# A two-layer decoder trunk on one core: VectorE in program order, weight units split two ahead, and the first four projection tiles summed slice by slice of x

## The chip, the core and the metric

The kernel runs on one core of a Trainium2 chip. The metric is device time in microseconds (us): the median of the runs of one program. One more execution is profiled, and its trace is what the rows below come from.

## The reference, cut to what matters

The input x is 256 tokens of 2048 values; all data are fp32. Two layers follow one another, and a last RMSNorm closes the program:

```python
for l in range(2):
    h = rmsnorm(x, mix_norm_g[l])
    pa, pb, pc, pd = split(h @ w_in[l])            # one projection, four groups of columns
    ya = gated_mlp(pa)                             # layer norm over v, causal 128x128 mixing
    yb = rwkv7(pb)                                 # p += (previous token - p) * mu, then the delta rule
    yc = block_attention(pc)                       # rotary q and k, softmax
    yd = gated_linear_attention(pd)
    x = x + concat(ya, yb, yc, yd) @ w_out[l]
    u = causal_conv3(rmsnorm(x, ffn_norm_g[l]) @ w_up[l])
    gate, up = split(u)
    x = x + (silu(gate) * up) @ w_down[l]          # inner width 5632
return rmsnorm(x, final_norm_g)
```

## The kernel before, in words

**Weights.** All weights come as one stream `ws` of 776 units; a unit is 128 x 1024 fp32 (512 KB) and holds 8 blocks of 128 x 128. SP issues the loads into 4 buffers `raw`. Each unit is split in two halves: ScalarE casts a half to H (fp32r, L182), VectorE subtracts, L = raw - H (L183); H and L have 7 buffers each. TensorE makes three products for each block, H with the high part of the activation, H with its low part, L with the high part (L219 to L221; wide forms L206 to L209 and L240 to L242). `proj` sums 16 blocks, that is two units, to one tile of 128 x 256 in PSUM.

**Order.** Only TensorE's order is the written one. The other engines' instructions are placed by a scheduler; the splits carry a priority of 3000, so they go in front of whatever else is ready on ScalarE and VectorE. Each call of `unit()` (L173) splits the unit and calls `pump()` (L150), which runs one step of each live generator: the mixers' work (`b_pre`, `b_grams`, `b_vt`, `solve`, `d_scores`, `c_rope`, `c_score`, `a_mix`) is written as generators, and TensorE gets a step's matmuls between two units.

**Start.** x is loaded in four pieces of 4 slices (a slice is 128 features of all 256 tokens), the first piece in two halves with the halves of unit 0 between; then come units 1 to 5 and a table `cst`. `x_ready` (L248) turns a slice into its high part on ScalarE (L255) and its low part on VectorE (L90, the helper `stt`). `x_square` (L258) sums the squares for the norm on ScalarE and VectorE, some odd slices on GpSimd; `rms_gen` (L286) sums them over features on TensorE (L293), takes the power on GpSimd (L298) and spreads the row scale to `rb` (L304, L306). Four projection tiles follow one another, each summed over all 16 slices, units 0 to 7.

**Group B of the projection.** `shift` (L348) is one token's mixing with the one before: VectorE multiplies by `rb` (L351), ScalarE scales (L352), VectorE adds the shifted part (L90). The first tiles go to `act12`, `pm13`, k and r, then v. `b_pre` (L375) prepares decay and gates, `b_grams` (L480) makes the norms: a reduction (L505), a transfer to DRAM (`tN`, L508) and back (L511) issued by GpSimd, and then 15 pairs of a product (L518) and a sum (L520), growing from 1 to 225 elements. `solve` (L567) inverts by squaring: matmul (L576), product (L591), add (L595).

**Feed-forward.** For each of 44 inner tiles a round makes two wide projections, `conv` on each (VectorE L1070, ScalarE L1072, two L90 on VectorE), Silu, a product (L1101), and the split of the result (L1103, L1104).

Of the kernel before, what the change touches and what calls it, by code (L numbers as in the profile page):

```python
# [10 lines left out]
F32 = mybir.dt.float32  # L11
# [41 lines left out]
def trunk_kernel(ctx: ExitStack, tc: tile.TileContext, x, ws, ph, pf, pm, pa, pb, cs, out, depth=DEPTH):  # L53
    nc = tc.nc
# [70 lines left out]
    for n in range(2, 4):  # L125
        raws[n] = load_raw(n)
    for n in range(4, 6):
        raws[n] = load_raw(n)
# [42 lines left out]
    ust = {"u": 0, "ev": None, "blk": 8, "H": None, "L": None}  # L171

    def unit():  # L173
        u = ust["u"]
        raw = raws.pop(u) if u in raws else load_raw(u)
        H, L = [], []
        for n in range(2):
# [7 lines left out]
            L.append(l)  # L185
        ust["u"] = u + 1
        ust["blk"] = 0
        ust["H"], ust["L"] = H, L
        pump()
        return H, L  # L190

    def block():
# [3 lines left out]
        ust["blk"] = b + 1  # L196
        w = slice((b % 4) * 128, (b % 4 + 1) * 128)
# [60 lines left out]
    def x_square(k, pool=False, final=False):  # L258
# [61 lines left out]
    with tc.high_priority(offset=3000):  # L320
        for k in range(16):
            x_ready(k, phs[0], PF_MIXG)
    with tc.high_priority(offset=2962):
        for k in range(16):
            x_square(k, True)

    for layer in range(depth):
# [958 lines left out]
```

## Time and profile before

| | us |
|---|---|
| median of 3 runs | 2379.26 |
| lowest and highest | 2378.59, 2380.8 |
| profiled execution | 2378.92 |
| its span in the trace | 2377.2 |
| TensorE busy | 2354.7 (99%) |
| VectorE busy | 1765.9 (74%) |
| ScalarE busy | 1349.5 (57%) |
| GpSimd busy | 99.4 (4%) |

The span runs from the first to the last instruction; 1.72 us of the execution lie around it. A busy share is an average over stages, and matmul ends are modelled. The times at which TensorE starts its instructions, and the waits that the trace puts down to a releaser, say where it loses time.

### The profile page before, as it was taken

Reading aid. Unit: us, or ns where it says so; the run is one execution under the profiler, and the core shown is the slowest. Engines: PE = TensorE matmul, PEld = TensorE weight load, DVE = VectorE, ACT = ScalarE, POOL = GpSimd, SP = SyncE. Lnnn points to the kernel's source line nnn. Section 1 sums busy time; section 2 is a strip of 40 time slices with the busy share of each in tenths; the row PEclk is TensorE's granted clock in tenths of the full one; section 3 lists DMA queues with packets and bytes.
Section 4 is the critical chain, followed back from the end, with each engine's and each line's share of the span. In section 5 each row is a group of like instructions: output and inputs, shape, how many; then the busy total and the mean of one; then the engine's idle time right before and its main releaser. Section 6 shows DMA issues by size and latency. Waiting matters only on the chain.

```text
span 2377.2 us, 39934 instructions
## 1 busy us (share of the span) xinstructions
PE 2354.7 (99%) x14764; PEld 2058.6 (87%) x14764; DVE 1765.9 (74%) x3471; ACT 1349.5 (57%) x2605; POOL 99.4 (4%) x134
## 2 busy tenths in 40 slices
PE   8999999999999999999999999999999999999998
PEld 8987888988888888888899788889888888888887
DVE  7886677787875588787668867777888756788764
ACT  6654456566654466665565444556666545666654
POOL 3110100000000000000011011000000000000000
PEclk9999999999999999999999999999999999999999
DMA  7553455555555555555655434455555555555553
GB/s 242 172 180 105 140 180 186 187 186 186 186 186 191 191 186 186 187 186 199 208 176 185 152 107 166 171 186 187 186 186 186 186 188 187 190 188 187 185 180 132
DMA packets 117859, 426.81 MB, mean 180 GB/s; under 512 B 13376, under 2 KB 13520, under 8 KB 117536
## 3 DMA queue, kind: packets, MB, share of 16 engines
q1 hardware_dynamic: 114144, 412.38, 50.0%
q0 software_dynamic: 3520, 11.89, 1.8%
q8 instruction: 115, 1.88, 0.3%
q14 instruction: 80, 0.66, 0.1%
HBM read 419.50 MB, written 4.72 MB: 178 GB/s over the span
## 4 chain that ended last, share of the span: by engine, by line
PE 98%; DVE 1%; DMA 0%; ACT 0%; issue 0%; POOL 0%; SPq 0%; POOLq 0%; ACTq 0%; DVEq 0%
PE mm L207 47%; PE mm L206 23%; PE mm L240 4%; PE mm L242 4%; PE mm L241 4%; PE mm L219 3%; PE mm L221 3%; PE mm L220 3%; PE mm L209 1%; PE mx L642 1%; PE mx L576 1%; PE mx L541 1%; DMA ab<-in_x_dram 0%; PE mx L923 0%; PE mx L832 0%; PE mx L952 0%
## 5 line engine op out<-in xcount | busy, mean ns | idle before, releaser
L182 ACT CAST H<-raw 128x512 fp32r<-128x512 f32 x1552 | 959.0, 620 | 916.0 <-PE mm L207 654.0
L183 DVE TENSOR_TENSOR L<-raw,H 128x512 fp32r<-128x512 f32 x1552 | 1074.9, 694 | 521.5 <-ACT H L182 503.5
L207 PE MATMUL mm<-xa,H 128*128 128x512 f32 x3008 | 1050.0, 397 | 0.0
L206 PE MATMUL mm<-xa,L 128*128 128x256 f32 x2820 | 792.9, 281 | 0.0
L207 PEld LDWEIGHTS mm<-xa,H 128*128 128x128 f32 x3008 | 553.1, 188 | 120.6
L207 PE MATMUL mm<-s,H 128*128 128x512 f32 x1560 | 544.1, 395 | 0.1
L206 PEld LDWEIGHTS mm<-xa,L 128*128 128x128 f32 x2820 | 531.6, 188 | 8.8
L206 PE MATMUL mm<-s,L 128*128 128x256 f32 x1470 | 413.1, 281 | 0.0
L207 PEld LDWEIGHTS mm<-s,H 128*128 128x128 f32 x1560 | 286.9, 188 | 60.8 <-DVE s L1104 1.0
L206 PEld LDWEIGHTS mm<-s,L 128*128 128x128 f32 x1470 | 277.4, 189 | 4.1
L90 DVE SCALAR_TENSOR_TENSOR w1k<-w1k,pft,w1k 128x255 f32<-128x255 f32 x352 | 169.1, 480 | 13.4
L240 PE MATMUL mm<-H,xa 128*128 128x512 f32 x384 | 159.4, 415 | 0.0
L219 PE MATMUL mm<-xa,H 128*128 128x256 f32 x512 | 150.0, 293 | 7.2 <-ACT H L182 6.3
L242 PE MATMUL mm<-L,xa 128*128 128x512 f32 x384 | 152.4, 397 | 0.0
L241 PE MATMUL mm<-H,xa 128*128 128x512 f32 x384 | 152.1, 396 | 0.0
L221 PE MATMUL mm<-xa,L 128*128 128x256 f32 x512 | 146.2, 286 | 1.2 <-DVE L L183 1.2
L220 PE MATMUL mm<-xa,H 128*128 128x256 f32 x512 | 146.5, 286 | 0.3 <-DVE xa L90 0.3
L219 PEld LDWEIGHTS mm<-xa,H 128*128 128x128 f32 x512 | 98.7, 193 | 8.0 <-ACT H L182 6.3
L1072 ACT ACTIVATE w1k<-w1k,pft 128x256 f32<-128x256 f32 x176 | 104.8, 595 | 0.1
L221 PEld LDWEIGHTS mm<-xa,L 128*128 128x128 f32 x512 | 98.6, 192 | 1.8 <-DVE L L183 1.8
L220 PEld LDWEIGHTS mm<-xa,H 128*128 128x128 f32 x512 | 98.6, 192 | 1.3 <-DVE xa L90 1.0
L240 PEld LDWEIGHTS mm<-H,xa 128*128 128x128 f32 x384 | 72.5, 189 | 20.8 <-issue 3.6
(298 smaller groups left out, 2165.5 us busy)
## 6 DMA issues: line engine op xcount, KB each, us to landing
raw<-in_ws_dram SPq DMA_DIRECT2D x775, 512.0 KB, 3.3
s<-in_pb_dram POOLq DMA_DIRECT2D x10, 256.0 KB, 5.3
ab<-in_x_dram POOLq DMA_DIRECT2D x4, 512.0 KB, 6.0
xscr<-ab POOLq DMA_DIRECT2D x4, 512.0 KB, 5.0
ab<-xscr POOLq DMA_DIRECT2D x4, 512.0 KB, 5.9
ab<-in_x_dram SPq DMA_DIRECT2D x3, 512.0 KB, 8.4
out_dram<-s SPq DMA_DIRECT2D x3, 512.0 KB, 4.5
cst<-in_cs_dram SPq DMA_DIRECT2D x1, 1040.5 KB, 7.2
```

Of the source, the lines that this page charges most:

```text
L90: return V.scalar_tensor_tensor(out=o, in0=a, scalar=s, in1=b, op0=op0, op1=op1)
L182: S.copy(h, src)
L183: V.tensor_sub(l, src, h.bitcast(F32))
L206: T.matmul(ps[:, :256], L, a[:, 0, :], start=False, stop=False)
L207: T.matmul(ps, H, a.rearrange("p s n -> p (s n)"), start=(k == 0), stop=(k == n - 1))
L219: T.matmul(o, H, a[:, 0, :], start=(k == 0), stop=False)
L220: T.matmul(o, H, a[:, 1, :], start=False, stop=False)
L221: T.matmul(o, L, a[:, 0, :], start=False, stop=(k == n - 1))
L240: T.matmul(ps[t], ah[:, ts], H[k % 2], start=(k == 0), stop=False)
L241: T.matmul(ps[t], al[:, ts], H[k % 2], start=False, stop=False)
L242: T.matmul(ps[t], ah[:, ts], L[k % 2], start=False, stop=(k == n - 1))
L1072: S.activation(acc, hr, AF.Identity, scale=cw(2), bias=cw(3))
```

## The change

1. VectorE joins TensorE in the written order: what stands in the program first runs first, and a priority no longer moves anything on it.
2. The split is a function of its own, `split(u)`; `unit()` takes a split that is made already, pumps the mixers, and then splits ahead up to two units (`look`, 2 after the first four tiles, 0 before).
3. x comes in pieces of 1, 1, 2, 2, 2, 4 and 4 slices between the units. `first_tiles()` sums four tiles slice by slice, in two banks of PSUM; the program that prepares the weights reorders the first units so that each holds the blocks of two slices for four tiles. Squares are taken two slices at a time on ScalarE and added on VectorE; the squares on GpSimd go. Ten fp32 matmuls on a zeroed tile stand ahead of everything on TensorE.
4. In layer 0 `rms_gen` starts one step earlier in units of half the length (`fine`), the tables `hb` and `selrk` are made behind it, and the tiles of `act12`, `pm13`, k0 and k1 are the first four, k2 the fifth.
5. Steps of mixers move: `b_pre`'s scans wait for k3; the exponentials of `b_grams`' input are fetched one ahead; `b_vt` has a wait more; `d_scores`' preparation has two parts; the softmax's scaling comes a step later (`c_scale`); `a_mix` has one yield between its power and its use of it; in the feed-forward the product and the split of round j come inside round j+1 (`gate2`, `gate3`), and both convolutions stand behind the second projection.

```diff
-    load_x(1, x, nc.sync)
-    raws[1] = load_raw(1)
-    for n in range(2, 4):
-        load_x(n, x, nc.sync)
...
+    for n in range(1, 4):
+        first_x(2 * n, 2)
         raws[n] = load_raw(n)
+    for c in range(2, 4):
+        first_x(4 * c, 4)
...
+    busy = slot("s13", [256])
+    V.memset(busy, 0.0)
...
-    ctx.enter_context(tc.manual_schedule(engines={mybir.EngineType.PE}))
+    ctx.enter_context(tc.manual_schedule(engines={mybir.EngineType.PE, mybir.EngineType.DVE}))
+    wps = mx()
+    for n in range(10):
+        T.matmul(wps[:, :128], busy[:, :128], busy[:, 128:256], start=True, stop=True)
...
+    def unit():
+        u = ust["u"]
+        if u not in splits:
+            split(u)
         ust["u"] = u + 1
         ust["blk"] = 0
-        ust["H"], ust["L"] = H, L
+        H, L = ust["H"], ust["L"] = splits.pop(u)
         pump()
+        for v in range(u + 1, min(u + 1 + ust["look"], 2 * depth * NW)):
+            if v not in splits:
+                split(v)
         return H, L
...
+        for k in range(16):
+            if k % 2 == 0:
+                ready(k + 2)
+                split(k // 2 + 1)
+                ready(k + 3)
+                with tc.high_priority(offset=2962):
+                    x_square2(k, acc)
+            hls = [block() for n in range(4)]
+            if k < 14:
+                for n in range(4):
+                    step(n, k, hls[n])
+            else:
+                late.append(hls)
+        for n in range(4):
+            for d in range(2):
+                step(n, 14 + d, late[d][n])
+        ust["look"] = 2
...
-        o = proj(xacts())
-        o13 = proj(xacts())
-        ok0 = proj(xacts()) if layer == 0 else None
+        early = list(outs0) if layer == 0 else []
...
+        early += [proj(xacts()) for _ in range(1 if layer == 0 else 2)]
+        ust["fine"] = False
         drain(gR)
+        o, o13 = next_b(), next_b()
...
-                ga = conv(pg, 2 * j)
-                ua = conv(pu, 2 * j + 1)
+                cg, cu = conv(pg, 2 * j), conv(pu, 2 * j + 1)
+                ga, ua = conv2(*cg), conv2(*cu)
                 S.activation(ga, ga, AF.Silu)
-                V.tensor_mul(ga, ga, ua)
                 gt[j] = gcur[:, jj]
-                S.copy(gt[j][:, 0, :], ga)
-                V.tensor_sub(gt[j][:, 1, :], ga, gt[j][:, 0, :].bitcast(F32))
+                pend = (j, ga, ua)
```

**VectorE at the start.** Before, a row is L90 for a slice's low part, L183 for a weight half and L274 for a sum of squares:

```order
L90 SCALAR_TENSOR_TENSOR xa_111<-ab_1_79,pht_76,xa_111 128x256 x2
L183 TENSOR_TENSOR L_224<-raw_80,H_223 128x512
L90 SCALAR_TENSOR_TENSOR xa_116<-ab_1_79,pht_76,xa_116 128x256 x2
L183 TENSOR_TENSOR L_228<-raw_80,H_227 128x512
L274 TENSOR_TENSOR acc_19_151<-acc_19_151,w1k_155 128x256
L90 SCALAR_TENSOR_TENSOR xa_121<-ab_3_85,pht_76,xa_121 128x256 x2
L90 SCALAR_TENSOR_TENSOR xa_126<-ab_3_85,pht_76,xa_126 128x256 x2
L183 TENSOR_TENSOR L_256<-raw_87,H_255 128x512
```

After, L194 is the weight half and L287 the sum of squares of two slices:

```order
L90 SCALAR_TENSOR_TENSOR xa_129<-ab_1_79,pht_76,xa_129 128x256
L194 TENSOR_TENSOR L_133<-raw_83,H_132 128x512
L194 TENSOR_TENSOR L_137<-raw_83,H_136 128x512
L90 SCALAR_TENSOR_TENSOR xa_129<-ab_1_79,pht_76,xa_129 128x256
L90 SCALAR_TENSOR_TENSOR xa_142<-ab_1_79,pht_76,xa_142 128x256
L194 TENSOR_TENSOR L_146<-raw_89,H_145 128x512
L194 TENSOR_TENSOR L_150<-raw_89,H_149 128x512
L90 SCALAR_TENSOR_TENSOR xa_142<-ab_1_79,pht_76,xa_142 128x256
```

Weight halves and slices alternate from the first slice on, two halves for two slices, where slices 4 to 15 stood before the second and third unit's halves.

**VectorE behind the first tiles.** Before, L351 and L90 are a shift's two steps, L749 to L759 copies and fills for the gates, and L183 stands between them:

```order
L351 TENSOR_TENSOR w1k_438<-mm_222,rb_429 128x256
L183 TENSOR_TENSOR L_586<-raw_583,H_585 128x512
L183 TENSOR_TENSOR L_590<-raw_583,H_589 128x512
L90 SCALAR_TENSOR_TENSOR s_44_213<-w1k_438,pft_197,s_44_213 128x256
L351 TENSOR_TENSOR w1k_448<-mm_287,rb_429 128x256
L183 TENSOR_TENSOR L_636<-raw_633,H_635 128x512
L749 COPY s_44_213<-s_44_213 32x256
L96 TENSOR_SCALAR sg_215<-s_44_213 96x256
L90 SCALAR_TENSOR_TENSOR s_44_213<-w1k_448,pft_197,s_44_213 128x256
L183 TENSOR_TENSOR L_640<-raw_633,H_639 128x512
```

After, the shift's steps are L409 and L90, its first column's fill L408:

```order
L408 MEMSET w1k_607 128x1
L409 TENSOR_TENSOR w1k_607<-mm_128,rb_539 128x256
L90 SCALAR_TENSOR_TENSOR s_75_470<-w1k_607,pft_463,s_75_470 128x256
L408 MEMSET w1k_613 128x1
L409 TENSOR_TENSOR w1k_613<-mm_128,rb_539 128x256
L90 SCALAR_TENSOR_TENSOR s_75_470<-w1k_613,pft_463,s_75_470 128x256
L408 MEMSET w1k_619 128x1
L409 TENSOR_TENSOR w1k_619<-mm_482,rb_539 128x256
L90 SCALAR_TENSOR_TENSOR s_75_470<-w1k_619,pft_463,s_75_470 128x256
L194 TENSOR_TENSOR L_629<-raw_626,H_628 128x512
```

Five shifts, from the one of `act12` (eleven rows further up) to the one of k2 (`w1k_619`), stand in one row ahead of the halves of unit 12 (`L_629` and the next).

**VectorE around unit 46 of layer 0.** Before, L884 to L890 are the rotary step of one input (two tokens' halves), and the norms' pairs L518 and L520 are long done:

```order
L884 TENSOR_TENSOR w2k_2027<-mm_1749,rope_433 128x512
L885 TENSOR_TENSOR w2k_2028<-mm_1749,rope_433 128x512
L183 TENSOR_TENSOR L_2137<-raw_2134,H_2136 128x512
L889 TENSOR_TENSOR s_402_2026<-w2k_2027,w2k_2028 128x8x32
L890 TENSOR_TENSOR s_402_2026<-w2k_2028,w2k_2027 128x8x32
L884 TENSOR_TENSOR w2k_2033<-mm_1750,rope_433 128x512
L183 TENSOR_TENSOR L_2141<-raw_2134,H_2140 128x512
L885 TENSOR_TENSOR w2k_2034<-mm_1750,rope_433 128x512
L183 TENSOR_TENSOR L_2177<-raw_2174,H_2176 128x512
L889 TENSOR_TENSOR s_402_2026<-w2k_2033,w2k_2034 128x8x32
```

After, L976 to L982 are the rotary step, L584 and L586 the norms' pairs:

```order
L194 TENSOR_TENSOR L_1993<-raw_1990,H_1992 128x512
L194 TENSOR_TENSOR L_1997<-raw_1990,H_1996 128x512
L976 TENSOR_TENSOR w2k_2013<-mm_1748,rope_583 128x512
L977 TENSOR_TENSOR w2k_2014<-mm_1748,rope_583 128x512
L981 TENSOR_TENSOR s_397_2012<-w2k_2013,w2k_2014 128x8x32
L982 TENSOR_TENSOR s_397_2012<-w2k_2014,w2k_2013 128x8x32
L976 TENSOR_TENSOR w2k_2019<-mm_1749,rope_583 128x512
L977 TENSOR_TENSOR w2k_2020<-mm_1749,rope_583 128x512
L981 TENSOR_TENSOR s_397_2012<-w2k_2019,w2k_2020 128x8x32
L982 TENSOR_TENSOR s_397_2012<-w2k_2020,w2k_2019 128x8x32
L584 TENSOR_TENSOR w1k_2028<-s_322_1710 128x81
L586 TENSOR_REDUCE s_322_1710<-w1k_2028 128x9
```

The halves at the top are those of unit 45. Between them and the next L194 (unit 46) there stand the whole rotary step, four pairs of the norms (81 to 144 elements) and one copy; before, one or two such instructions stood between two halves.

## Rows read from the trace of the kernel before

**Rows 1.** The page's part 4, the chain of work that ended last, share of the span by engine.

```profile
PE 98%; DVE 1%; DMA 0%; ACT 0%; issue 0%; POOL 0%; SPq 0%; POOLq 0%; ACTq 0%; DVEq 0%
```

**Rows 2.** The waits of TensorE over the whole span: engine, tile and line that waited, what ended the wait; us in total, times, longest.

```profile
PE mx L576 <- DVE s L591: 3.0, 4, 0.8
PE mm L221 <- DVE L L183: 1.2, 2, 0.7
```

**Rows 3.** The timeline of TensorE (PE) from the first product to the end of the fourth projection tile: start in us, duration, line, operation, out<-in, shape, count; in brackets the idle time before and what ended it. L219, L220 and L221 are the three products of a block; L293 is the column sum of the squares.

```profile
6.33 0.58 PE L219 MATMUL mm<-xa,H 128*128 128x256 f32 x1 [6.33 <-ACT H L182]
...
14.60 0.58 PE L220 MATMUL mm<-xa,H 128*128 128x256 f32 x1 [0.35 <-DVE xa L90]
...
18.82 0.41 PE L221 MATMUL mm<-xa,L 128*128 128x256 f32 x1
19.03 0.32 PE L219 MATMUL mm<-xa,H 128*128 128x256 f32 x1
...
19.31 0.28 PE L221 MATMUL mm<-xa,L 128*128 128x256 f32 x1
19.42 0.28 PE L219 MATMUL mm<-xa,H 128*128 128x256 f32 x1
...
29.62 0.28 PE L293 MATMUL mx<-ones,acc 128*128 128x1 f32 x2
...
30.43 0.36 PE L219 MATMUL mm<-xa,H 128*128 128x256 f32 x1
...
39.13 0.28 PE L221 MATMUL mm<-xa,L 128*128 128x256 f32 x1
```

**Rows 4.** The timeline of VectorE (DVE) over 5 to 36 us, same columns.

```profile
14.07 3.24 DVE L90 SCALAR_TENSOR_TENSOR xa<-ab,pht,xa 128x256 fp32r<-128x256 f32 x8
...
24.87 0.42 DVE L274 TENSOR_TENSOR acc<-acc,w1k 128x256 f32<-128x256 f32 x1
25.21 2.49 DVE L183 TENSOR_TENSOR L<-raw,H 128x512 fp32r<-128x512 f32 x4
...
30.61 0.16 DVE L296 TENSOR_SCALAR sm<-mx 128x2 f32<-128x2 f32 x1 [1.36 <-PE mx L293]
```

**Rows 5.** The timeline of ScalarE (ACT) over 3 to 36 us, same columns: a cast of a weight half, the copy of the row scale rb, and the scaling inside a shift.

```profile
5.66 0.62 ACT L182 CAST H<-raw 128x512 fp32r<-128x512 f32 x1 [0.82 <-DMA raw<-in_ws_dram]
...
33.87 0.37 ACT L306 COPY rb<-mx 128x256 f32<-128x256 f32 x1
...
35.59 0.51 ACT L352 ACTIVATE s<-w1k,hb 128x256 f32<-128x256 f32 x1
```

**Rows 6.** The timeline of TensorE around layer 0's solve (L576), same columns; L240 to L242 are weight products.

```profile
193.09 0.65 PE L576 MATMUL mx<-s,ab 64*64 64x32 f32 x16 [0.70 <-DVE s L591]
194.56 1.59 PE L576 MATMUL mx<-s,ab 64*64 64x32 f32 x48 [0.82 <-DVE s L591]
...
197.11 0.63 PE L240 MATMUL mm<-H,xa 128*128 128x512 f32 x1
197.53 0.63 PE L241 MATMUL mm<-H,xa 128*128 128x512 f32 x1
```

**Rows 7.** Busy time in windows, the first just behind those two waits of layer 0, the second around the same place in layer 1: us, busy time (instructions) of each engine, the granted clock (PEclk) of the window, DMA share, GB/s.

```profile
196.00:200.00 4.00, 4.00 (x15) 3.19 (x13) 0.99 (x3) 0.62 (x1) 0.00 (x0) 0.57 0.00 0
...
1368.00:1372.00 4.00, 3.88 (x58) 3.46 (x59) 1.66 (x7) 0.62 (x1) 0.00 (x0) 1.00 0.08 28
```

**Rows 8.** VectorE's instructions of the first 700 us, grouped by line and shape: count | busy us, mean ns | idle before. L351 and L90 are the two VectorE steps of a shift.

```profile
L90 DVE SCALAR_TENSOR_TENSOR s<-w1k,pft,s 128x256 f32<-128x256 f32 x14 | 6.7, 476 | 0.0
...
L351 DVE TENSOR_TENSOR w1k<-mm,rb 128x256 f32<-128x256 f32 x14 | 5.7, 416 | 0.6 <-PE mm L221 0.6
```

**Rows 9.** The timeline of GpSimd (POOL) over 115 to 135 us: the two transfers of the norms to DRAM and back.

```profile
121.21 1.23 POOL L508 DMA_DIRECT2D tN<-s  x1 [6.62 <-DVE s L505]
127.45 0.56 POOL L511 DMA_DIRECT2D s<-tN  x1 [5.01 <-DVE L L183]
```

**Rows 10.** VectorE's instructions between 136 and 154 us, grouped by line: count | busy us, mean ns | idle before. This is the sequence of products and sums over the norms.

```profile
L518 DVE TENSOR_TENSOR w1k<-s 128x1 f32<-128x1 f32 (+14 forms) x15 | 4.5, 301 | 0.2
L520 DVE TENSOR_REDUCE s<-w1k 128x1 f32<-128x1 f32 (+14 forms) x15 | 3.5, 235 | 0.2
```

**Rows 11.** The timeline of VectorE inside the rotary step of layer 0.

```profile
156.40 0.68 DVE L884 TENSOR_TENSOR w2k<-mm,rope 128x512 f32<-128x512 f32 x1
...
158.20 0.42 DVE L889 TENSOR_TENSOR s<-w2k,w2k 128x256 f32<-128x256 f32 x1
158.53 0.42 DVE L890 TENSOR_TENSOR s<-w2k,w2k 128x256 f32<-128x256 f32 x1
```

**Rows 12.** The timeline of TensorE: the first products of units 28, 32, 42 and 46 of layer 0 (counted by the first use of a new H tile in the order of the instructions).

```profile
106.10 0.39 PE L207 MATMUL mm<-xa,H 128*128 128x512 f32 x1
...
120.29 0.48 PE L207 MATMUL mm<-xa,H 128*128 128x512 f32 x1
...
150.97 0.39 PE L240 MATMUL mm<-H,xa 128*128 128x512 f32 x1
...
163.76 0.48 PE L240 MATMUL mm<-H,xa 128*128 128x512 f32 x1
```

**Rows 13.** Busy time in a window inside the feed-forward part, columns as in rows 7 with all engines.

```profile
1000.00:1010.00 10.00, 10.00 (x58) 8.69 (x57) 8.31 (x18) 5.89 (x12) 0.00 (x0) 1.00 0.54 201
```

**Rows 14.** ScalarE's instructions of the first 700 us, grouped by line and shape: the first step of the feed-forward's convolution.

```profile
L1072 ACT ACTIVATE w1k<-w1k,pft 128x256 f32<-128x256 f32 x44 | 26.2, 596 | 0.0
```

More of the change, by code (lines that the diff above doesn't have):

```diff
@@ L169, in lockstep, with split @@
             yield 1
-    ust = {"u": 0, "ev": None, "blk": 8, "H": None, "L": None}
-    def unit():
-        u = ust["u"]
+    ust = {"u": 0, "ev": None, "blk": 8, "H": None, "L": None, "fine": False, "look": 0}
+    splits = {}
+    def split(u):
         raw = raws.pop(u) if u in raws else load_raw(u)
@@ L256, in x_ready, with x_square2, first_tiles, step @@
         stt(xl, xt, g, xh.bitcast(F32), OP.mult, OP.subtract)
[L258 removed]
+    def x_square2(k, acc):
+        xt = X[k // 4][:, k % 4:k % 4 + 2, :].rearrange("p a n -> p (a n)")
+        if k == 0:
+            S.activation(acc, xt, AF.Square)
+        else:
+            q = w2k()
+            S.activation(q, xt, AF.Square)
+            V.tensor_add(acc, acc, q)
+    def first_tiles():
+        accw = slot("s16", [4, 256])
+        acc = accw[:, 0:2, :].rearrange("p a n -> p (a n)")
+        acc2[0], accp[0] = accw[:, 0, :], accw[:, 1, :]
+        banks = [mmt(), mmt()]
+        outs = [banks[n // 2][:, (n % 2) * 256:(n % 2) * 256 + 256] for n in range(4)]
+        def step(n, k, hl):
+            a = xacts1(k)
+            H, L = hl
+            T.matmul(outs[n], H, a[:, 0, :], start=(k == 0 and n % 2 == 0), stop=False, skip_group_check=True)
+            T.matmul(outs[n], H, a[:, 1, :], start=False, stop=False, skip_group_check=True)
+            T.matmul(outs[n], L, a[:, 0, :], start=False, stop=(k == 15 and n % 2 == 1), skip_group_check=True)
+        late = []
+        def ready(k):
+            if k < 16:
+                with tc.high_priority(offset=3000):
+                    x_ready(k, phs[0], PF_MIXG)
+            if k == 11:
+                ust["pool"] = G.tensor_copy(sm(1), X[2][:, 3, 0:1])
+        ready(0)
+        split(0)
+        ready(1)
+        for k in range(16):
[9 more added lines that the diff above has]
+                    step(n, k, hls[n])
+            else:
+                late.append(hls)
[3 more added lines that the diff above has]
+        ust["look"] = 2
+        return outs
+    def x_square(k, final=False):
         xt = X[k // 4][:, k % 4, :]
@@ L318, in to_T @@
             yield 1
[L320 to L325, printed above, removed]
+    outs0 = first_tiles()
     for layer in range(depth):
@@ L423, in b_pre @@
             S.activation(az, az, AF.Ln, bias=1.0)
+            yield from wait("k3")
+            yield 1
             for i in range(2):
@@ L454, in b_pre, with exps @@
             rkp = slot("s7", [4, 256])
-            for i in range(4):
-                yield from wait(f"r{i}")
-                V.tensor_mul(rkp[:, i, :], bR[:, i, :], bK[:, i, :])
+            def exps(i):
                 ep = w1k(260)[:, :258].rearrange("p (c n) -> p c n", c=2)
@@ L462, in b_pre @@
                     S.activation(en[:, c, :], cum[:, i, 128 * c + 1:128 * c + 129], AF.Exp, scale=KAPPA, bias=kcr[:, 1, i, c:c + 1])
+                return ep, en
+            nxt = exps(0)
+            for i in range(4):
+                yield from wait(f"r{i}")
+                V.tensor_mul(rkp[:, i, :], bR[:, i, :], bK[:, i, :])
+                ep, en = nxt
+                if i < 3:
+                    nxt = exps(i + 1)
                 def v2(a):
@@ L557, in b_vt @@
             have["vT"] = vT
+            yield from wait("bt")
             btk = slot("s7", [2, 512])
@@ L761, in trunk_kernel @@
         for i in range(4):
-            shift(ok0 if i == 0 and layer == 0 else proj(xacts()), 6 + i, bK[:, i, :])
+            shift(next_b(), 6 + i, bK[:, i, :])
             S.activation(sq[:, i, :], bK[:, i, :], AF.Square, scale=pft[:, PF_KK + i:PF_KK + i + 1])
```

101 lines of the change are left out of this document (70 added, 31 removed).

## The prediction

> **What bounds the kernel now.** I read the chain of waits first: 98% of what ended last is TensorE's own work [rows 1], so a change pays only where TensorE waits or runs slowly. The list of its waits comes next. Behind the first product it is short: 3.0 us before the solve's matmuls, 1.2 us for a low weight half [rows 2]. So at most three places can give time back: the start, the two solves, and what is lost to a low clock behind waits. From some 40 us on TensorE is otherwise fed without a gap, by a scheduler that puts every split first. The change takes that preference away on VectorE, so the other question is where TensorE will wait for a half that it now gets in time.
>
> **The start (gain).** First product 6.33, last product of the fourth tile 39.13 [rows 3]. [...] With 0.12 for the last, the tiles end at 39.25; 0.81 us between 29.62 and 30.43 went to the norm's sums [rows 3], which only move, so the tiles cost time up to 38.4. After the change TensorE needs 192 products: 192 x 0.12 = 23.0 us. The first half of unit 0 has been in the core since 5.66 [rows 5]; one slice less is loaded ahead of it, so I take a first product at 5.7 (no later than today's 6.33). VectorE's queue: a slice's low part each 0.40 (eight in 3.24), a half each 0.60 (four in 2.49, 0.69 alone) [rows 4], a sum of two squares, 512 wide, priced like a half: 16 x 0.40 + 16 x 0.60 + 7 x 0.60 = 20.2 us, less than 23.0, so TensorE sets the end. ScalarE's, with the eight squares of two slices that it takes over from GpSimd in part, is like VectorE's and also below 23: 16 scalings near 0.41, 16 casts near 0.52 and 8 squares near 0.6 are 19.7, an estimate from the one cast of 0.62 alone and the steps behind one another [rows 5]. The loads on GpSimd's queue that waited for its squares (the tables of group B) now wait for one small copy behind slice 11, and `cst` goes ahead of unit 6 on SP's queue; their users come at 34 us and later, so both cost nothing here. For the waits on pieces still under way I take what the start shows today for the same two inputs, 0.35 [rows 3] + 1.2 [rows 2] = 1.6. End at 5.7 + 23.0 + 1.6 = 30.3; gain 38.4 - 30.3 = **8.1**, bounded above by no waits (9.7).
>
> [...] The ten zero matmuls run in time in which TensorE has nothing to do (before 5.7), so they cost nothing unless they end late. [...]
>
> **The solve (gain).** Two waits in each layer, 3.0 us together [rows 2], because splits stand in front of L591 on VectorE. With the splits two units ahead, the squaring's steps need not queue behind them; what is late next there is TensorE's own work. In layer 0 the waits of 0.70 and 0.82 are followed by products 0.42 apart [rows 6] and by a granted clock of 0.57 over the next 4 us [rows 7]: the low level, 0.19 more for each of 8 products (spacing at full clock about half of 0.42 and a little, 0.23) = 1.5. In layer 1 the clock stays at 1.00 [rows 7]. All of it: **4.5**; bounds 1.5 (waits halved, clock still falls) and 4.5.
>
> **Five shifts in a row (loss).** Before, weight halves went between them. Now five shifts stand ahead of the halves of unit 12. A shift is L351, ScalarE's step, L90, each waiting for the one before: 0.42 + 0.51 + 0.48 = 1.4 [rows 5, 8], five 7.0, and with the tables, copies and fills some 10 short ones at 0.35 (an estimate) 10.5 us. They can start when the row scale is there. Today that took from the last sum of squares, 25.2, to 34.2 [rows 4, 5], 9 us; in the new start the last sum is at about 25 and the same steps come one half unit apart: 33.8. So unit 12's first low half is made at 33.8 + 10.5 + 0.6 = 44.9. TensorE gets there after two tiles more, 30.3 + 96 x 0.12 (11.5) + 1.7 for norm sums, transposes and group B's first matmuls = 43.5. Wait **1.4**; bounds 0 and 3.5 (ScalarE's step behind casts in each shift).
>
> **Units 28 to 31 (loss).** VectorE's written list between halves is a shift, a product for the gate and four steps of the norm's inputs, eight operations of 256 columns, then five, alternately: 13.5 us with the halves over four units, and TensorE passes them in 120.29 - 106.10 = 14.2 [rows 12]. Under 1 us of slack over four units does not cover its waits for ScalarE's exponentials. I take **1.0**, bounds 0 and 2.
>
> **Norms and rotary step, layer 0 (loss).** This is where order costs most. The last reduction of the norms comes later now, about 141.2 (three lists of 3.5 to 4 us behind units that pass in 2.8, from unit 36 on). The trip to DRAM and back stays: 121.21 to 127.45 for the first transfer [rows 9], and as long as its wait, 5.0, for the second: 11.2, back at 152.4. The pairs L518 and L520 (15 pairs, 8.0 us [rows 10], half of it in the last five) start 1.4 after their place came up, behind unit 42's start at 150.97 [rows 12]. Then, in order: 2.8 for four pairs and a copy and 1.2 for unit 44's halves, with a sum, until 156.4; 3.3 for four pairs, a difference and unit 45's halves until 159.7; the rotary step, four times 0.60 and four times 0.33 [rows 4, 11] = 3.7, four pairs 2.6, a copy 0.4 and the first half of unit 46, 0.6, until 167.0. TensorE needs that half 0.5 behind unit 46's start at 163.76 [rows 12], at 164.3: wait **2.8** (about 1.4 if the norms are back in time; 5.5 if each list is a third longer). Nothing covers it: the two units of lead are 5.6 us, this list alone 7. In layer 1 the two steps do not meet; **0.5**.
>
> **A low clock behind the new waits (loss).** Of two places with a pair of waits of 0.7 to 0.8 us, one was followed by the low level for 1.5 us' worth [rows 6, 7]. Three new waits of 1.0 to 2.8 in layer 0: one such fall, **1.5**; bounds 0 and 4.5.
>
> **Feed-forward (nothing).** A round is two projections of about 5.7 us. VectorE has 8 halves of 0.60 and ten other steps of 0.33 to 0.40, 8.4 of 11.4 us (busy 8.3 of 10.0 now, which counts overlaps [rows 13]). Behind the second projection the order has the sum, both convolutions with ScalarE's 0.60 [rows 14] between, 4.2 in all, and then a unit's halves, 1.2 at most: 5.4, needed 5.7 later. It holds, by 0.3 to 1.1. The moves in d_scores, c_scale, a_mix and b_vt change what waits on VectorE inside lists that have slack; they cost nothing as long as two units of lead cover them.
>
> **Sum.** 8.1 + 4.5 - 1.4 - 1.0 - 2.8 - 0.5 - 1.5 = 5.4 off. The profiled execution took 2378.92 (2377.2 span and 1.72 around it, untouched), 0.34 under the median of the runs, inside their spread: 2378.92 - 5.4 = **2373.5**.
>
> [...] Two operations on VectorE without a wait between them start 0.60 apart though one lasts 0.69 [rows 4]. [...]
>
> **Rivals.** (1) *VectorE's order costs what the start gives.* For it: lists of 7 us against a lead of 5.6, and three places at their upper bounds (3.5, 2, 5.5) with two falls of the clock (3.0) and layer 1's 0.5 make 14.5 against 12.6: 2377 to 2381, within the bound. Against it: each upper bound needs ScalarE to be late at every step. [...] (3) *No new stall.* The lists fit better than I count, only the two gains stay, less 2 to 4: 2367 to 2370. (4) *The feed-forward's order becomes the bound, slower.* One mechanism: the run behind the second projection lasts over 5.7 us, because ScalarE's step, behind two casts (0.62 each [rows 5]), is late. From then on each of 88 rounds pays the excess; 0.1 to 0.2 us a round is 9 to 18: 2382 to 2391. Against it: 0.3 to 1.1 us in hand. [...]
>
> **How the numbers follow.** Forecast 0.50 (2370.5 to 2376.5, most of it under 2374.5), rival 1 0.23, rival 2 0.07, rival 3 0.10, rival 4 0.08, rival 5 0.02. A measurement of this kernel tells 0.2%, 4.8 us, from no change: faster is under 2374.5, slower over 2384. Faster: 0.44 of the forecast and rival 3, 0.54. Slower: rival 4 without its lowest end, 0.07. Same: the rest, 0.39. The range leaves out rival 4, the lowest of rival 3 and the highest of rival 1: 2368 to 2379.5.
>
> **What would show it.** The fourth tile's end at 29 to 32 us with products 0.12 apart from the first; no wait of L576's successor for L591 in either layer; waits of TensorE for low halves near 44, 110 and 165 us, of 1 to 3 us each, and the granted clock below 1.00 behind one of them; no such wait from 700 to 1200 us. I am wrong in the gain if the first products start 0.21 apart, in the losses if the list of waits names no low half behind 40 us, and altogether if one shows up in each feed-forward round.

## The result and the profile after

The changed kernel takes 2410.41 us (median of 4 runs, 2409.93 to 2416.38) against 2379.86 for the kernel before on the same chip: 1.0134 times as long, 95% interval 1.0122 to 1.0146, some 30.6 us **slower**. The forecast was 2373.5, the range 2368 to 2379.5. Its span is 2408.4 us.

The chain of work that ended last, by engine and by line, now has VectorE, the weight loads and ScalarE in it [compare rows 1]; L229 and L228 are the wide products, L194 is the low weight half, L193 the cast:

```profile
PE 88%; DVE 6%; DMA 3%; ACT 2%; issue 1%; POOL 0%; SPq 0%; ACTq 0%; POOLq 0%; DVEq 0%
PE mm L229 42%; PE mm L228 20%; PE mm L262 3%; PE mm L264 3%; PE mm L263 3%; DMA raw<-in_ws_dram 3%; PE mm L241 2%; PE mm L242 2%; PE mm L243 2%; PE mm L231 2%; DVE w1k L90 2%; DVE L L194 2%; PE mx L709 1%; PE mx L643 1%; PE mx L607 1%
```

TensorE's waits over the whole span; before, the list was short [rows 2]. The solve's waits for L591 (now L658) are gone. These are the eight largest groups, four of them for L194, the low half of a unit:

```profile
PE mm L231 <- DVE L L194: 7.6, 13, 1.6
PE mm L228 <- DVE L L194: 6.4, 4, 1.7
PE mm L243 <- DVE L L194: 2.1, 2, 1.5
PE mm L264 <- DVE L L194: 2.1, 2, 1.3
PE mx L922 <- DVE w2k L897: 1.8, 1, 1.8
PE mx L620 <- DVE s L90: 1.7, 1, 1.7
PE mx L541 <- DVE s L525: 1.6, 1, 1.6
PE mx L919 <- DVE w2k L894: 1.6, 1, 1.6
```

A wait in this list is not the whole loss, since a product behind a gap lasts longer too (0.38 or 0.39 us in the lines below, against 0.28). What the start of each unit's first product shows (after minus before, in us, worked out from the two traces by the order of the H tiles) is where the time went:

| first product of unit | 8 | 12 | 46 | 54 | 76 | 92 | 124 | 212 | 214 | 388 | 416 | 480 | 512 | 736 |
|---|---|---|---|---|---|---|---|---|---|---|---|---|---|---|
| after minus before | -6.7 | -7.3 | +2.2 | -4.0 | +2.6 | +2.9 | +4.1 | +9.2 | +11.1 | +16.3 | +19.7 | +18.9 | +20.6 | +31.3 |

Some of it is work of TensorE that now stands at another unit (four matmuls of `b_pre` moved from unit 8 to 12, the solve from 50 to 54). At unit 76 that is over: the start's gain of 5 to 6 us and the solve's have been used up. From unit 124 to 388, layer 0's feed-forward, 12.3 us go, in layer 1 (512 to 736) 10.7.

**The start.** TensorE's timeline, columns as in rows 3; L158 are the zero matmuls, L299 to L301 the products of the first tiles:

```profile
1.19 4.36 PE L158 MATMUL mx<-s 128*128 128x128 f32 x20 [1.19 <-DVE s L152]
5.79 0.39 PE L299 MATMUL mm<-xa,H 128*128 128x256 f32 x1 [0.24 <-ACT H L193]
...
6.86 0.28 PE L300 MATMUL mm<-xa,H 128*128 128x256 f32 x1
6.97 0.28 PE L301 MATMUL mm<-xa,L 128*128 128x256 f32 x1
...
8.61 0.39 PE L300 MATMUL mm<-xa,H 128*128 128x256 f32 x1 [0.53 <-DVE xa L90]
...
10.59 0.39 PE L299 MATMUL mm<-xa,H 128*128 128x256 f32 x1 [0.42 <-ACT H L193]
...
26.46 0.39 PE L299 MATMUL mm<-xa,H 128*128 128x256 f32 x1 [0.34 <-ACT H L193]
```

The products start 0.12 us apart from the second block on, the spacing that was forecast. But unit 8 starts at 33.2, not at 30.3: there are waits of 0.53 for a slice's low part and 0.42 and 0.34 for casts, and units 4 to 7 pass in 13.5 us for 11.4 of products. ScalarE's timeline shows a cause for the later part of this, and when the row scale is ready:

```profile
25.79 1.14 ACT L193 CAST H<-raw 128x512 fp32r<-128x512 f32 x2 [2.58 <-DMA raw<-in_ws_dram]
...
37.58 0.37 ACT L377 COPY rb<-mx 128x256 f32<-128x256 f32 x1
```

The casts at 25.79 waited 2.58 us for a weight load. VectorE then makes the five shifts (L409, L90) and the halves of unit 12:

```profile
33.06 2.49 DVE L194 TENSOR_TENSOR L<-raw,H 128x512 fp32r<-128x512 f32 x4
...
37.98 0.43 DVE L409 TENSOR_TENSOR w1k<-mm,rb 128x256 f32<-128x256 f32 x1
...
47.90 0.68 DVE L194 TENSOR_TENSOR L<-raw,H 128x512 fp32r<-128x512 f32 x1
```

The four L194 take 2.49 us, as before [rows 4]: they start 0.60 apart, though one alone lasts 0.69 (at 5.77), so the price of 0.60 for a half held.

**The mixers of layer 0.** TensorE's new waits in order of time: unit 12, the first group B transposes behind the exponentials (L620), the first matmul of group D's scores (L919), a half near unit 46, and group D's scores again (L922):

```profile
48.63 0.38 PE L243 MATMUL mm<-xa,L 128*128 128x256 f32 x1 [1.52 <-DVE L L194]
...
106.82 0.33 PE L620 MATMUL mx<-cst,s 128*128 128x128 f32 x1 [1.72 <-DVE s L90]
...
139.61 1.16 PE L919 MATMUL mx<-w2k,w2k 64*128 64x128 f32 x16 [1.55 <-DVE w2k L894]
...
168.06 0.51 PE L264 MATMUL mm<-L,xa 128*128 128x512 f32 x1 [1.34 <-DVE L L194]
...
172.43 1.11 PE L922 MATMUL mx<-w2k 64*128 64x64 f32 x16 [1.76 <-DVE w2k L897]
```

Behind the last two the difference to the kernel before stands at +5.7 (unit 48), its highest in layer 0's mixers. Windows behind these two waits and behind one in layer 1, columns as in rows 7. After waits of 1.3 and 1.8 us the clock stayed at 1.00, in layer 1 it fell once, to 0.57 over 4 us:

```profile
172.00:176.00 4.00, 3.57 (x29) 3.17 (x30) 4.00 (x8) 2.27 (x5) 1.29 (x2) 1.00 0.46 146
...
1288.00:1292.00 4.00, 4.00 (x22) 4.00 (x23) 2.60 (x7) 0.62 (x1) 0.00 (x0) 0.57 0.31 97
```

That holds for this one trace. In those of e1 to e8 below the clock fell near unit 46 every time, in e3 to 0.81 and 0.76 (160 to 164 and 164 to 168 us), in e6 to 0.61 and 0.53 (the same two windows); e4, with waits of 1.2 and 1.8 us at the same two places, has this window:

```profile
172.00:176.00 4.00, 3.41 (x23) 3.13 (x24) 4.00 (x9) 1.26 (x3) 1.45 (x2) 0.62 0.41 122
```

From unit 46 to 48 the changed kernel loses 3.5 us, and e2, e4, e5, e7 and e8 lose 4.8 to 5.4.

**The feed-forward.** One of the waits, on ScalarE (casts L193, copy of a finished tile's upper half L247), VectorE (sum L248, split L1200, convolutions L1174 and L90, halves L194) and TensorE:

```profile
553.28 1.14 ACT L193 CAST H<-raw 128x512 fp32r<-128x512 f32 x2 [2.45 <-DMA raw<-in_ws_dram]
555.24 0.62 ACT L193 CAST H<-raw 128x512 fp32r<-128x512 f32 x1 [0.82 <-DMA raw<-in_ws_dram]
555.76 0.37 ACT L247 COPY w1k<-mm 128x256 f32<-128x256 f32 x1
```

```profile
550.30 2.49 DVE L194 TENSOR_TENSOR L<-raw,H 128x512 fp32r<-128x512 f32 x4
556.16 0.42 DVE L248 TENSOR_TENSOR w1k<-w1k,mm 128x256 f32<-128x256 f32 x1 [3.37 <-ACT w1k L247]
...
559.76 2.49 DVE L194 TENSOR_TENSOR L<-raw,H 128x512 fp32r<-128x512 f32 x4
```

```profile
553.63 0.28 PE L231 MATMUL mm<-xa,L 128*128 128x256 f32 x1
...
560.50 0.38 PE L231 MATMUL mm<-xa,L 128*128 128x256 f32 x1 [1.07 <-DVE L L194]
```

The tile that L247 copies was finished before 553.63, where the next tile's second product starts. The copy ran at 555.76, behind three casts, of which the first two began as a load landed and the third waited 0.82 for the next. VectorE, in written order, stood 3.37 us at L248 with all the halves of the next units behind it, and the half that TensorE wanted at 559.4 came at 560.4. Over the program ScalarE's casts waited for loads

```profile
ACT H L193 <- DMA raw<-in_ws_dram: 208.1, 188, 2.9
```

where they had waited 5.7 us, 2 times, in the kernel before. A load (L110) waits for a free raw buffer, and a buffer is free when VectorE has made its low halves. SP's waits that end with such a half, in the changed kernel and then in the kernel before:

```profile
SPq L110 <- DVE L L194: 1964.1, 734, 11.8
```

```profile
SPq L110 <- DVE L L183: 1289.4, 495, 7.1
```

So there is a loop: late halves, late loads, late casts, a late copy, late halves.

The ends of the four halves of the feed-forward are a second place. The last round's product (L1196) and split (L1200) have no round to hide in, VectorE waits for ScalarE in between, and the halves come last:

```profile
709.71 0.42 DVE L1196 TENSOR_TENSOR w1k<-w1k,w1k 128x256 f32<-128x256 f32 x1
710.60 0.43 DVE L1200 TENSOR_TENSOR s<-w1k,s 128x256 fp32r<-128x256 f32 x1 [0.47 <-ACT s L1197]
710.94 2.49 DVE L194 TENSOR_TENSOR L<-raw,H 128x512 fp32r<-128x512 f32 x4
```

```profile
711.68 0.38 PE L228 MATMUL mm<-tt,L 128*128 128x256 f32 x1 [1.60 <-DVE L L194]
```

### The profile page after: what moved, and what is told of

It is laid out like the page before. It is cut to its first block, busy times and chain, and to the rows that moved or that the text cites. A ratio compares the mean times of both kernels' runs of the same rounds, so it can differ in the third digit from the quotient of the medians.

```text
span 2408.4 us, 39614 instructions
## 1 busy us (share of the span) xinstructions
PE 2368.7 (98%) x14784; PEld 2052.6 (85%) x14784; DVE 1716.2 (71%) x3470; ACT 1356.2 (56%) x2603; POOL 99.4 (4%) x124
## 4 chain that ended last, share of the span: by engine, by line
PE 88%; DVE 6%; DMA 3%; ACT 2%; issue 1%; POOL 0%; SPq 0%; ACTq 0%; POOLq 0%; DVEq 0%
PE mm L229 42%; PE mm L228 20%; PE mm L262 3%; PE mm L264 3%; PE mm L263 3%; DMA raw<-in_ws_dram 3%; PE mm L241 2%; PE mm L242 2%; PE mm L243 2%; PE mm L231 2%; DVE w1k L90 2%; DVE L L194 2%; PE mx L709 1%; PE mx L643 1%; PE mx L607 1%
## 5 line engine op out<-in xcount | busy, mean ns | idle before, releaser
L193 ACT CAST H<-raw 128x512 fp32r<-128x512 f32 x1552 | 948.8, 618 | 857.3 <-PE mm L229 384.9
L229 PE MATMUL mm<-xa,H 128*128 128x512 f32 x3008 | 1048.8, 396 | 0.0
L194 DVE TENSOR_TENSOR L<-raw,H 128x512 fp32r<-128x512 f32 x1552 | 989.4, 690 | 70.9 <-ACT H L193 69.0
L228 PE MATMUL mm<-xa,L 128*128 128x256 f32 x2820 | 792.7, 281 | 0.0
L229 PEld LDWEIGHTS mm<-xa,H 128*128 128x128 f32 x3008 | 552.9, 188 | 119.8
L229 PE MATMUL mm<-s,H 128*128 128x512 f32 x1560 | 543.7, 395 | 0.0
L228 PEld LDWEIGHTS mm<-xa,L 128*128 128x128 f32 x2820 | 531.7, 189 | 5.6
L228 PE MATMUL mm<-s,L 128*128 128x256 f32 x1470 | 413.0, 281 | 0.0
L229 PEld LDWEIGHTS mm<-s,H 128*128 128x128 f32 x1560 | 287.0, 188 | 59.8
L228 PEld LDWEIGHTS mm<-s,L 128*128 128x128 f32 x1470 | 277.4, 189 | 3.9
L248 DVE TENSOR_TENSOR w1k<-w1k,mm 128x256 f32<-128x256 f32 x188 | 78.4, 417 | 220.8 <-ACT w1k L247 198.1
L90 DVE SCALAR_TENSOR_TENSOR w1k<-w1k,pft,w1k 128x255 f32<-128x255 f32 x352 | 162.3, 482 | 35.6 <-ACT w1k L1176 29.4
L241 PE MATMUL mm<-xa,H 128*128 128x256 f32 x448 | 130.1, 290 | 0.0
L243 PE MATMUL mm<-xa,L 128*128 128x256 f32 x448 | 126.7, 283 | 2.1 <-DVE L L194 2.1
L242 PE MATMUL mm<-xa,H 128*128 128x256 f32 x448 | 126.6, 283 | 0.0
L1176 ACT ACTIVATE w1k<-w1k,pft 128x256 f32<-128x256 f32 x176 | 96.6, 595 | 35.6 <-DVE w1k L1174 34.7
L1159 DVE TENSOR_TENSOR ab<-ab,mm 128x256 f32<-128x256 f32 x90 | 37.9, 421 | 100.6 <-PE mm L229 100.6
L264 PEld LDWEIGHTS mm<-L,xa 128*128 128x128 f32 x384 | 72.0, 187 | 20.6 <-DVE L L194 3.1
## 6 DMA issues: line engine op xcount, KB each, us to landing
cst<-in_cs_dram SPq DMA_DIRECT2D x1, 1040.5 KB, 11.9
```

What stands on the lines that cost most here:

```text
L90: return V.scalar_tensor_tensor(out=o, in0=a, scalar=s, in1=b, op0=op0, op1=op1)
L193: S.copy(h, src)
L194: V.tensor_sub(l, src, h.bitcast(F32))
L228: T.matmul(ps[:, :256], L, a[:, 0, :], start=False, stop=False)
L229: T.matmul(ps, H, a.rearrange("p s n -> p (s n)"), start=(k == 0), stop=(k == n - 1))
L241: T.matmul(o, H, a[:, 0, :], start=(k == 0), stop=False)
```

## The experiments

Theory A: in the feed-forward the loop just told makes the loss. Rival B: VectorE's run behind the second projection is by itself too long for two units of lead (the prediction's rival 4, with a look at VectorE alone). A later theory, C, is on where the start's gain went.

Each kernel is set against the kernel before on its own chip; "more" is the difference of the two medians, and what an edit is worth is read from that column. Each kernel has one trace, and the traces differ in how often and how long the granted clock fell (once before the last unit in the changed kernel, three times in e1, two or three times in e2 to e10; its mean over the span is 0.998 in the changed kernel, 0.995 in e1, 0.996 in e5, e6 and e8, 0.997 in the others), also where an edit changes nothing. From unit 46 to 48 a fall is worth some 1.3 to 1.9 us by the figures above (an estimate), so differences of that size between two totals are set beside the unit starts.

| kernel | us | before on the same chip | more | ratio, 95% interval |
|---|---|---|---|---|
| the change | 2410.41 | 2379.86 | +30.6 | 1.0134 (1.0122 to 1.0146) |
| e1_half_loads | 2396.62 | 2380.43 | +16.2 | 1.007 (1.0055 to 1.0085) |
| e2_dve_copy | 2396.09 | 2380.43 | +15.7 | 1.007 (1.0053 to 1.0086) |
| e3_dve_scheduled | 2379.70 | 2380.43 | -0.7 | 0.9995 (0.9986 to 1.0004) |
| e4_ends | 2408.34 | 2380.43 | +27.9 | 1.0115 (1.0100 to 1.0130) |
| e5_no_warm, one run | 2424.34 | 2379.18 | +45.2 | |
| e6_start_alone | 2381.38 | 2379.18 | +2.2 | 1.0008 (0.9999 to 1.0017) |
| e7_copy_ends | 2393.34 | 2379.18 | +14.2 | 1.0058 (1.0045 to 1.0072) |
| e8_raw5 | 2397.80 | 2379.18 | +18.6 | 1.0076 (1.0062 to 1.0089) |
| e9_catch_up | 2375.55 | 2379.29 | -3.7 | 0.9983 (0.9974 to 0.9992) |
| e10_order_catch_up | 2389.37 | 2379.29 | +10.1 | 1.0043 (1.0029 to 1.0057) |

**Half of the loads (e1).**

```diff
-        raw = raws.pop(u) if u in raws else load_raw(u)
+        if u in raws:
+            raw = raws.pop(u)
+        elif u % (2 * NW) >= 124 and u % 2 == 1:
+            raw = held[0]
+        else:
+            raw = load_raw(u)
+        held[0] = raw
```

> Leaves work out: in the feed-forward every second weight unit is not loaded, its split reads the unit before once more, so that four raw buffers hold eight units. Theory A (in the feed-forward VectorE's written order frees the raw buffers late, ScalarE's casts wait for the loads, its copy of a finished tile waits behind the casts, and VectorE waits for the copy): the waits for a low half inside the up projections go, the four at the ends of the halves (about 2 us each) stay: 2410.4 - 16 = 2394. Theory B (the run of sum, two convolutions and ScalarE's step on VectorE is by itself too long for two units of lead): the waits stay, 2410.

Measured 2396.62, 14.4 less than the change (+16.2 against +30.6). In the trace the difference to the kernel before stays the same from unit 124 to 212 (+8.7 at both; +4.1 to +9.2 in the changed kernel), and steps at the ends of the halves. ScalarE's waits for loads fall from 208 us to

```profile
ACT H L200 <- DMA raw<-in_ws_dram: 23.5, 24, 3.0
```

So the waits inside the up projections hang on the loads, not on the length of VectorE's run: A, against B. (The +8.7 stands there before the edit does anything: in this trace the granted clock fell once more, at unit 12, and was low for longer near unit 46; its mean is 0.995 against 0.998.)

**The copy on VectorE (e2).**

```diff
-        S.copy(o, ps[:, 256:])
+        V.tensor_copy(o, ps[:, 256:])
```

> The copy of a finished wide tile's upper half goes from ScalarE to VectorE, nothing else changes; VectorE gets 0.4 us more per tile. Theory A: VectorE no longer waits behind casts that wait for loads, 2395 to 2400. Theory B: VectorE's run gets longer, TensorE waits more, 2415 or above.

2396.09, 14.9 less. Again nothing is lost from unit 124 to 212 (+5.9 at both), though casts still wait 130 us for loads and VectorE has 0.4 us more to do for each tile. With e1 this closes the loop from its other side: late loads and late casts don't hurt by themselves, the copy has to stand behind them, as it does at 555.76 in the changed kernel, behind three casts.

**Five raw buffers (e8).**

```diff
-    rawp = ctx.enter_context(tc.tile_pool(name="rawp", bufs=4))
-    hp = ctx.enter_context(tc.tile_pool(name="hp", bufs=7))
+    rawp = ctx.enter_context(tc.tile_pool(name="rawp", bufs=5))
+    hp = ctx.enter_context(tc.tile_pool(name="hp", bufs=6))
```

> Five raw buffers in place of four, and six buffers for H and six for L in place of seven, so that it fits; nothing else changes. Theory A: a load gets one unit more of time, the casts stop waiting for loads, most of the up projections' loss goes: 2398 to 2402. If the depth of the raw buffers is not what makes the casts late, or the seventh H buffer carries the lead: 2410 or above.

2397.80, 11.9 less, just under A's 2398, with every load made. Six H buffers also keep the casts from running so far ahead, so this one does not separate the two; but the casts' waits for loads are gone, and from unit 124 to 212 nothing is lost. A rival, that the loads themselves are slower, falls too: from issue to landing a load takes 4.2 us (median) in the changed kernel and 3.3 in the kernel before, but also 4.1 here and 4.2 in e2.

```profile
ACT H L193 <- DMA raw<-in_ws_dram: 4.7, 4, 2.6
```

By the unit starts the two feed-forward parts lose 6.0, 5.7 and 6.2 us in e1, e2 and e8, against 23.0: the same 17 us are gone in all three. That the totals differ (14.4, 14.9 and 11.9) goes with what the mixers lose in each, as far as one trace each can tell.

**The ends of the halves (e4; with the copy on VectorE, e7).**

```diff
-            gate2(*pend)
-            gate3(*pend)
+            def tail(p):
+                yield 1
+                gate2(*p)
+                yield 1
+                gate3(*p)
+            spawn(tail(pend))
             pend = None
```

> The product and the split of a half's last round come at the next two unit boundaries, not at once. Both theories: the four waits of about 1.6 us (1.9 of time each) at the ends of the halves go, 2410.4 - 7.5 = 2403; the other waits stay.

2408.34: 2.6 less and not 7.5, and the two intervals overlap, so the total alone shows nothing. In the trace the four waits for a half (6.4 us) become 0.4 and four short ones for the split itself (1.4). By the unit starts each end costs 0.7 to 0.9 in place of 1.4 to 1.8 (units 212 to 215 and their like), and the feed-forward loses 18 us in place of 23. The total shows less of it, since the mixers of layer 0, which the edit does not touch, lose 1.8 more here (+5.9 at unit 124 against +4.1), where the clock fell (the window with 0.62 above).

> The copy on VectorE and the spread ends of the halves together, VectorE in written order. With the waits behind casts gone, the four end waits (1.2 to 1.4 us of time each with the copy on VectorE) go too: 2396 - 5 = 2391. What is left over the kernel before is then the mixers' and the projections into the residual.

2393.34, 1.5 less than e2, not 5, and the two intervals overlap. By the unit starts the ends cost 1.3 each with the copy on VectorE (units 212 to 214 in e2) and next to nothing in e7, where 0.1 to 0.3 is lost at the units behind; the two feed-forward parts lose 2.4 us in place of 5.7, which the totals do not show.

**VectorE scheduled (e3).**

```diff
-    ctx.enter_context(tc.manual_schedule(engines={mybir.EngineType.PE, mybir.EngineType.DVE}))
+    ctx.enter_context(tc.manual_schedule(engines={mybir.EngineType.PE}))
```

> All of the change, but VectorE is placed by the scheduler again (splits first), only TensorE keeps the written order. Both theories: the feed-forward's loss goes, and the new waits of the mixers for low halves too; the start's gain of about 7 stays, the solve's waits come back: 2370 to 2374. If the loss came from the new order of x, tiles and steps and not from VectorE's order, it stays above 2390.

2379.70: the whole loss of 30 us goes with VectorE's written order, but the gain does not come. Both theories missed that. Near unit 46 the trace has a wait of 2.4 us for the rotary step's result, and the difference to the kernel before goes from -8.1 at unit 14 to -3.4 at unit 76.

**The start alone (e6).** VectorE scheduled, and these written as before: `b_pre`'s scans, the exponentials, `b_vt`, `d_scores`, `c_scale`, `a_mix`, the feed-forward's rounds. The diff is the one of the change without those pieces, and without VectorE in the written order.

> The start alone: first tiles slice by slice, loads of x, early norm and zero matmuls as changed, but VectorE placed by the scheduler and the steps of the mixers and of the feed-forward written as before. Theory A: the start's gain of 5 to 6 us stays to the end, no new wait in the mixers: 2374.5. Rival (the early norm and the five shifts from the first tiles make the mixers late by themselves, also with VectorE scheduled): 2379.

2381.38, no gain either. The waits of TensorE name the place, the rotary step's result L962 ahead of L973:

```profile
PE mx L973 <- DVE s L962: 5.1, 2, 2.7
PE mx L634 <- DVE s L649: 1.5, 2, 0.8
```

The difference is -5.3 at unit 44 and +0.5 at unit 46. GpSimd's timeline shows the norms' transfers at 134.65 and 139.27, though TensorE is 5 us ahead there; before, they stood at 121.21 and 127.45 [rows 9]:

```profile
134.65 1.23 POOL L566 DMA_DIRECT2D tN<-s  x1 [1.37 <-DVE s L563]
139.27 0.55 POOL L569 DMA_DIRECT2D s<-tN  x1 [3.40 <-DMA tN<-s]
```

The order of TensorE's instructions explains it: `b_pre`'s first matmuls stand at unit 12 and not at 8, the norms' columns at 30 and not 26, the solve at 54 and not 50. The four first tiles are now ready together at unit 8, the fifth tile comes next, and group B's generator begins at unit 10 and not at 6; from then on it gets one step a unit. So group B is four units late, and its 15 pairs meet the rotary step, which isn't.

**Catching up (e9; on VectorE's written order, e10).** The two lines are what e9 adds to e6 and e10 adds to e7; with them the generators are pumped twice per unit from unit 10 to 13.

```diff
         gP = spawn(b_pre())
+        ust["fine"] = layer == 0
...
             shift(next_b(), 2 + i, bR[:, i, :])
+            ust["fine"] = False
```

> As the start alone, and in layer 0 the generators are pumped twice per unit from unit 10 to unit 13, so that group B's steps, which begin at unit 10 and not at 6 with the four tiles ready at once, are back at the units of the kernel before from unit 15 on. Theory C (the start's gain is given back because group B's steps run four units late and the norms' pairs meet the rotary step in front of unit 46): the waits there go, 2379.2 - 5.5 = 2374. Rival (VectorE is full from unit 13 to 46 whatever the order, so TensorE cannot come earlier): 2379 to 2381.

2375.55, 0.9983 of the kernel before: faster than both. The difference stays within 0.4 of -6.2 from unit 20 to 92; behind the start only the solve's old waits stay:

```profile
PE mx L634 <- DVE s L649: 3.0, 4, 0.8
```

Theory C holds, and its rival falls: VectorE was not full whatever the order. Of the 6.2, 3.9 are left at unit 736; 1.5 of the rest went behind the solve's waits (units 440 to 442), where the granted clock fell to 0.62 (1364 to 1368 us) and was 1.00 in the kernel before [rows 7].

> The same two pumps on the changed kernel with the copy on VectorE and the spread ends: VectorE in written order. Theory C: the waits at units 46 and 47 and the clock's fall there go, 2393.3 - 5 = 2388; the waits at units 13 to 33 stay, perhaps one unit earlier. Rival (the written order alone makes all the waits): 2393.

2389.37, 4.1 less than e7 where C expects 5. The two intervals overlap, though each of its four runs is faster than each of e7's; the waits ahead of the scores (L919, L922), the transposes (L620) and unit 46 are gone from the list. What is left over e9, 13.8 us, goes with VectorE's written order and its rearranged steps. The steps alone do not cost it: e3 has them with VectorE scheduled and stands at -0.7, e6 does not have them and stands at +2.2. Its waits are these, at group B's sums (L541) and for low halves at units 12 to 24 and where the output projection begins:

```profile
PE mx L541 <- DVE s L525: 4.1, 2, 2.5
PE mm L231 <- DVE L L194: 3.2, 4, 1.4
PE mm L243 <- DVE L L194: 2.4, 4, 1.0
```

**One zero matmul (e5).**

```diff
-    for n in range(10):
-        T.matmul(...)
+    T.matmul(...)
```

> One zero matmul in place of ten, else the changed kernel. If the ten raise the clock ahead of the first product: the first products start 0.21 apart for 4 us or more, and unit 8 starts 1.9 later than with ten (2 to 5 later). If they do nothing: the products start 0.12 apart as with ten and unit 8 starts at the same time within 0.3.

The products start 0.21 apart until 10.5, 5 us behind the first one:

```profile
5.27 0.58 PE L298 MATMUL mm<-xa,H 128*128 128x256 f32 x1 [3.28 <-ACT H L192]
...
6.59 0.41 PE L299 MATMUL mm<-xa,H 128*128 128x256 f32 x1
6.80 0.41 PE L300 MATMUL mm<-xa,L 128*128 128x256 f32 x1
...
10.63 0.28 PE L300 MATMUL mm<-xa,L 128*128 128x256 f32 x1
10.74 0.28 PE L298 MATMUL mm<-xa,H 128*128 128x256 f32 x1
```

Yet unit 8 starts as with ten (-6.9 against -6.7). The 1.9 that was expected is an estimate from the kernel before: 4.4 us, as from 14.60 to 19.03, hold 21 products at 0.21, each 0.09 more than 0.12 [rows 3]. With the ten the products stand closer from the second block on, but the first tiles do not end earlier by it: in both kernels the units from 4 on wait for casts and loads. The total of 2424.34 is one run; its feed-forward has 20 waits at the same instruction (L230, L231 in the changed kernel) in place of 10, which one run can't put down to the edit.

## Why the prediction was wrong

- **Feed-forward (nothing): this step failed.** "It holds, by 0.3 to 1.1" counted VectorE's run and one step of ScalarE. It did not follow what stands ahead of ScalarE's copy, nor that the raw buffers, and so the loads, hang on VectorE's halves. Measured: 23 us by unit starts, of which 14.9 (e2), 14.4 (e1) or 11.9 (e8) go with any link of that loop (17 by the unit starts, in all three); most of the rest is the ends of the halves (about 1.9 at unit 214), which I had not seen as a place at all. Rival 4 had the sign, the engine and a price of 9 to 18, at 0.08, but put the lateness on ScalarE's step in the convolution and not on the copy, and saw no loop.
- **Start, 8.1.** Mis-sized, and then mostly given back. Against 38.4, the tiles end at 33.2: 5.2. What waits cost is 4.5 us, not 1.6 (33.2 - 5.7 - 23.0): the list has 1.0 for casts, 0.9 for low halves and 0.8 for slices' low parts, and the product after one that waited starts 0.22 to 0.23 behind it and not 0.12 (8.61 to 8.83, 10.59 to 10.82). Of that, e6 shows that nothing is left at the end without the two extra pumps, and e9 that 3.7 is with them. The rival "VectorE's order costs what the start gives" did not name this: the steps begin four units later because their input tiles are ready later.
- **Zero matmuls at no cost, products 0.12 apart from the first.** They end at 5.55, and the first product, at 5.79, waited 0.24 for a cast: no cost. The products stand 0.12 apart from the second block on, as they do before behind 19.03 (0.11 to 0.12 [rows 3]). But it was worth nothing: e5 starts unit 8 at the same time.
- **The solve, 4.5.** Right, and near in size: by the unit starts 3.1 us in layer 0 (units 48 to 76) and 1.8 in layer 1 (440 to 441). In layer 1 VectorE's order is the cause: the waits are there in e3, e6 and e9, where it is scheduled, and gone in the changed kernel. In layer 0 it is one of two: e3 and e6 have no wait there either, with the solve four units later; at its old place e9 has two waits and e10 none, and e10 makes up 3.3 us on e9 between units 52 and 54.
- **Five shifts, 1.4.** 1.52 at 48.63. Both sides came some 3 us later than worked out, the half at 48.6 and not 44.9, TensorE at 46.5 and not 43.5; that the wait fits is luck, two errors of one size.
- **Units 28 to 31, 1.0.** A wait of 1.72 at 106.82 at the transposes, and 0.57 before it.
- **Norms and rotary step, 2.8.** 1.34 and 1.76 near units 46 and 47, and 1.6 at 139.6. Right place, but I ascribed the lateness of the norms to VectorE's lists; e9 shows that it is the generator's late beginning.
- **One fall of the clock, 1.5.** None in layer 0 (1.00) and one in layer 1 (0.57) in the trace of the changed kernel; in layer 0, where it was forecast, in each trace of e1 to e8 (to 0.62 in e4, to 0.53 in e6). So the term fits, and whether it is paid changes from trace to trace.
- **Outside the sum.** The output projection's beginning, 1 to 2 us in each layer (units 92 to 100 and 480 to 488), and group B's sums in layer 1 (3.3 at units 412 to 414, layer 1's fall of the clock to 0.57 in it) were not foreseen. Which pieces of VectorE's list cause the 13.8 us between e10 and e9 was not tried one by one and stays open.

The parts add up from the measured medians, each against the kernel before on its chip: the loop 14.9 (30.6 to 15.7, e2), the ends 1.5 (to 14.2, e7; 3.3 by the unit starts), group B's lateness 4.1 (to 10.1, e10), the rest of the written order with its steps 13.8 (to -3.7, e9).

## What to carry to other kernels

When an engine is taken from a scheduler that lets the supply go first, follow the whole loop and not its queue alone: which buffer its instruction frees, which load waits for the buffer, which engine waits for the load, and what else stands in that engine's queue. A lead of so many units is worth only as much as the input ring that feeds it (a fifth raw buffer took 11.9 us off, e8). And an earlier start counts only if the steps behind it begin earlier too (+2.2 in e6, -3.7 in e9): count at which unit each one begins, and what it meets there.

## What was unexpected of the hardware

With ten fp32 matmuls on zeros between 1.19 and 5.55 us the products start 0.12 us apart from the second block on, with one of them 0.21 apart until 10.5. With the same ten it varies from trace to trace: in e8 the products start 0.21 apart until 7.2. That this is the clock's doing is not shown: the trace of the changed kernel grants 1.00 in each window of 4 us from 0 to 16, and that of the kernel before 1.00 also over 5 to 19 us, where its products start 0.21 apart [rows 3] (columns as in rows 7 with all engines):

```profile
5.00:19.00 14.00, 11.42 (x45) 10.18 (x46) 11.94 (x23) 11.19 (x27) 8.46 (x11) 1.00 1.00 375
```

Waits of 1.3 and 1.8 us left the granted clock at 1.00 in layer 0 of the changed kernel and waits of 1.2 and 1.8 were followed by 0.62 in e4, while in the kernel before two waits of 0.7 and 0.8, with 64-row matmuls between them, were followed by 0.57 [rows 6, 7]; the length of the wait alone does not decide it.
